# Splitting half of the second gated weight set on GpSimd, in a two-layer decoder trunk

## The chip, the cores and the metric

The kernel runs on one core of a Trainium2 chip. The metric is the device time of one execution in microseconds, the median of three runs. Engines are called PE (TensorE), ScalarE (ACT), VectorE (DVE), GpSimd (POOL) and SP (SyncE, which issues the DMAs).

## What is computed

A decoder trunk of depth 2 for one sequence of 512 tokens with 1024 features, in float32: a layer with a diagonal state-space mixer and an MLP, then a layer with dilated attention and an MLP. Each sub-layer is an RMS norm, a shift and scale that come from a condition vector `c`, the mixer, a gate and a residual add. The place of the change is the end of the first mixer:

```python
z = jax.nn.gelu(y).astype(u.dtype)              # y: the state-space output, 512 x 1024
val, gate = jnp.split(z @ w_glu, 2, axis=-1)    # w_glu: 1024 x 2048
return val * jax.nn.sigmoid(gate)               # then h = h + gate_c * this
# ada_chunks, for each sub-layer: jax.nn.silu(c) @ w + b   (w: 1024 x 3072)
```

## The kernel before, in words

**Products in three parts.** A float32 product is made of three matmuls in a rounded format: each operand is split in a high half (the value rounded, a cast) and a low half (the value less its high half). For weights, `weights` (L811) loads 128 x 8 x 256 raw values by DMA, casts them to the high half `wh` (L828, on ScalarE) and subtracts to the low half `wl` (L830, on VectorE). For the activations, L773 is the cast (ScalarE) and L778 the subtraction (VectorE, or GpSimd for units 1 and 2). `linear_steps` (L842) issues, for each of eight k, high x high (L856), high weight x low activation (L857) and low weight x high activation (L858).

**The state-space mixer** (`ssm`, from L1626 on) works on four units of the features. A unit's end is: outputs on PE (L747, L751), copies (L753, ScalarE), transposes (L767, PE), gelu (L770, two per half, ScalarE), L773, L778. Unit ft gives the activations k = ft and k = ft + 4. VectorE's scans are L719, with products L710 to L716 ahead and L729 to L733 behind; those of unit 3 are in part on GpSimd (L729, L730).

**The gated product** (`glu`, L935) uses eight *sets* of weights, each 128 columns for the value and 128 for the gate, in the order k = 0, 4, 1, 5, 2, 6, 3, 7. So the matmuls of units 0, 1, 2 and 3 come in this order. Each set takes two PSUM banks of four (`mm_ps`, L79), so set n + 2 takes the banks of set n, which the sigmoid (L945, ScalarE) and L956 (VectorE) have read. Behind each set VectorE works on *ada jobs* (L1523, L1530 seven times, L1535, L1536): parts of the product of `c` with the ada weights of the next sub-layers, each with its own load of 1 MB (L1512).

**The first three sets** are made ready before `glu` begins (L1762). For them `weights` works in quarters: quarter i is k = i and i + 4. Of the tuple, the number for a set says how many of its quarters are cast and split on GpSimd; the others follow, by a given order, behind the copies of unit 3's kernel on ScalarE and the scan of unit 3 on VectorE. The raw loads of these sets wait for a mark on PE. From set 4 on, ScalarE casts and VectorE subtracts in two halves of 128 x 1024.

**What sets the order.** Up to L1760 the engines' orders are pinned as written. Around and behind it a scheduler orders each engine's instructions by a model of their times, so a change in one place can move others. Raw weights, high and low halves and ada loads all take tiles from one pool of 13 buffers (`W`), so each load waits, on SP's queue and in SP's order, for whoever last used its buffer.

Names in the built program: set 1 is W_1651 (raw), W_1654 (high), W_1655 (low); set 2 is W_1664, W_1667, W_1668; set 3 W_1677, W_1680, W_1681; set 4 W_1831, W_1834, W_1835; set 5 W_1840, W_1843, W_1844; set 6 W_1932, W_1935, W_1936; set 7 W_2024, W_2027, W_2028. Unit 3's activations are uz_215, unit 1's uz_195.

Of the kernel before, what the change touches and what calls it, by code (L numbers as in the profile page):

```python
# [94 lines left out]
class Trunk:  # L95
# [1646 lines left out]
    def run(self):  # L1742
        nc, a = self.nc, self.a
        stop = getattr(self, "stop", None)
        self.jobs_started = False
        self.job_mark, self.heads = None, False
        self.jobs, self.ends, self.mark, self.pe_mark, self.pending = [], [], None, None, []
        self.late, self.loaded = [], None
        self.r, self.rcol, self.columns_only = [None] * 2, [None] * 2, False
        self.stream, self.ready = self.weight_stream(), []  # L1750
        self.setup()
        self.z = [None] * KT
        self.unit = [None] * 4
        pool, dve = nc.gpsimd, nc.vector
        self.ssm_params()
        with self.pinned():
            gate0 = self.ssm(pool, dve)

        def ada(n, c0, c1, late=False):

            return self.ada_jobs(a["ada_w"][n // 2, n % 2][:, c0 * D:c1 * D], (c1 - c0) * D, n, c0, late)
        self.prefetch(3, (2, 0, 0))  # L1762
        self.side(0)
        ada1 = ada(1, 0, 2)
        self.glu(gate0)
        if stop == "h1":
            return
        self.side_rest()
        gate1 = ada(1, 2, 3)
        adakv = self.ada_jobs(a["kv_ada_w"], 2 * D, None, 0)  # L1770
        ada2 = ada(2, 0, 2)
        self.mlp(0, ada1[:, 0:8], ada1[:, 8:16], gate1)
        if stop == "h2":
            return
        self.side_rest()
        self.masks()
        gate2, ada3, gate3 = ada(2, 2, 3, True), ada(3, 0, 2, True), ada(3, 2, 3, True)
        self.attention(ada2, adakv, gate2)
        if stop == "h3":
            return  # L1780
        self.columns_only = True
        self.mlp(1, ada3[:, 0:8], ada3[:, 8:16], gate3)
        if stop == "h4":
            return
        while len(self.pending) > 1:
            self.pump()
        self.final(1)[0]()
# [34 lines left out]
```

## Time and profile before

| | before |
|---|---|
| median of 3 runs | 1546.73 us (1542.74 to 1547.42) |
| the profiled execution | 1544.54 us, its span 1542.8 us |
| PE busy | 1466.8 us, 95% of the span |
| VectorE busy | 926.1 us, 60% |
| ScalarE busy | 569.5 us, 37% |
| GpSimd busy | 108.9 us, 7%, nearly all of it in the first 175 us |
| mean granted clock of PE | 0.987 |

A busy share is a mean over stages with different limits. In the first 140 us the state-space mixer keeps VectorE at work and PE waits often; from the gated product on PE is nearly always busy. In the timelines below a row is one group of equal instructions that follow each other: start, length, engine, line, operation, tiles, shape and count, and in brackets the idle time of the engine before it and what ended it. A clock of 1.00 is the higher of PE's two levels, 2.4 GHz, and 0.50 the lower.

### The profile page before, as it was taken

The numbers are of one execution on the slowest core, as the hardware profiler recorded it, in microseconds if no ns is written. First come the engines' busy times: TensorE is split into PE (matmuls) and PEld (weight loads), VectorE is DVE, ScalarE is ACT, GpSimd is POOL, SyncE is SP. The second block draws the span as 40 slices with busy tenths as digits, with TensorE's granted clock in tenths as the row PEclk, the third lists the DMA queues.
The fourth block names the chain that finished last, engine by engine and source line by source line (L and its number), as shares of the span: only waits on it lengthen the run. The fifth ranks groups of instructions, "written<-read, shape, count | busy, mean of one in ns | idle before, by whom it ended". The sixth has DMA issues, their size and how long they took to land. (4 is left out here: it accounts for less than half of the span.)

```text
span 1542.8 us, 27284 instructions
## 1 busy us (share of the span) xinstructions
PE 1466.8 (95%) x11654; PEld 1230.6 (80%) x11654; DVE 926.1 (60%) x1657; ACT 569.5 (37%) x990; POOL 108.9 (7%) x94
## 2 busy tenths in 40 slices
PE   4847899999999999999999999999999999999998
PEld 3636789888888888987987888888778888888887
DVE  7898896989874345636656756533558534334332
ACT  6738533424142234423322322332435423232222
POOL 7582000000000000000000000000000000000000
PEclk9978999999999999999999999999999999999999
DMA  9413671976743333233444444222334333232301
GB/s 216 152 55 84 198 221 40 323 228 191 228 135 107 104 116 96 82 88 114 139 129 144 138 125 143 83 56 72 117 91 135 94 98 109 82 110 84 107 1 55
DMA packets 214489, 188.61 MB, mean 122 GB/s; under 512 B 7480, under 2 KB 208352, under 8 KB 214368
## 3 DMA queue, kind: packets, MB, share of 16 engines
q1 hardware_dynamic: 214368, 186.87, 40.2%
q8 instruction: 91, 1.49, 0.4%
q14 instruction: 30, 0.25, 0.1%
HBM read 182.66 MB, written 4.19 MB: 121 GB/s over the span
## 5 line engine op out<-in xcount | busy, mean ns | idle before, releaser
L828 ACT CAST W<-W 128x1024 fp32r<-128x1024 f32 (+1 forms) x228 | 223.6, 1031 | 391.9 <-PE mm L857 204.3
L856 PE MATMUL mm<-uz,W 128*128 128x512 f32 (+1 forms) x952 | 360.0, 381 | 1.9 <-ACT uz L773 1.7
L858 PE MATMUL mm<-uz,W 128*128 128x512 f32 (+1 forms) x952 | 358.3, 377 | 3.1 <-DVE W L830 3.1
L857 PE MATMUL mm<-uz,W 128*128 128x512 f32 (+1 forms) x952 | 358.1, 376 | 3.2 <-DVE uz L778 2.9
L830 DVE TENSOR_TENSOR W<-W,W 128x1024 fp32r<-128x1024 f32 (+1 forms) x228 | 266.5, 1196 | 151.2 <-ACT W L828 122.8
L856 PE MATMUL mm<-hid,W 128*128 128x512 f32 (+1 forms) x792 | 298.7, 378 | 0.9 <-ACT hid L1029 0.6
L857 PE MATMUL mm<-hid,W 128*128 128x512 f32 (+1 forms) x792 | 296.1, 374 | 2.7 <-DVE hid L1030 2.7
L858 PE MATMUL mm<-hid,W 128*128 128x512 f32 (+1 forms) x792 | 295.4, 373 | 0.0
L858 PEld LDWEIGHTS mm<-uz,W 128*128 128x128 f32 x952 | 179.8, 189 | 36.2 <-DVE W L830 3.5
L856 PEld LDWEIGHTS mm<-uz,W 128*128 128x128 f32 x952 | 179.7, 189 | 35.9 <-ACT uz L773 2.1
L857 PEld LDWEIGHTS mm<-uz,W 128*128 128x128 f32 x952 | 179.8, 189 | 35.3 <-DVE uz L778 3.2
L857 PEld LDWEIGHTS mm<-hid,W 128*128 128x128 f32 x792 | 149.1, 188 | 29.4 <-DVE hid L1030 3.8
L856 PEld LDWEIGHTS mm<-hid,W 128*128 128x128 f32 x792 | 148.8, 188 | 28.8 <-issue 1.4
L858 PEld LDWEIGHTS mm<-hid,W 128*128 128x128 f32 x792 | 149.0, 188 | 26.6
L881 DVE SCALAR_TENSOR_TENSOR h<-mm,ada,h 128x512 f32<-128x512 f32 (+1 forms) x77 | 54.1, 707 | 148.4 <-PE mm L858 148.4
L1530 DVE SCALAR_TENSOR_TENSOR aacc<-W,cs,aacc 128x256 f32<-128x256 f32 x196 | 96.4, 492 | 4.0
L1056 ACT ACTIVATE sg<-mm 128x512 f32<-128x512 f32 x60 | 35.6, 595 | 112.9 <-PE mm L858 111.1
L1058 DVE TENSOR_TENSOR sg<-sg 128x512 f32<-128x512 f32 x64 | 43.7, 687 | 54.1 <-ACT uz L1057 53.9
L1282 PE MATMUL mm<-W,hid 128*128 128x256 f32 x256 | 73.5, 287 | 0.0
L1283 PE MATMUL mm<-W,hid 128*128 128x256 f32 x256 | 72.4, 283 | 0.0
L1284 PE MATMUL mm<-W,hid 128*128 128x256 f32 x256 | 72.4, 283 | 0.0
L1155 ACT ACTIVATE sg<-aux,st 128x192 f32<-128x192 f32 (+3 forms) x64 | 36.7, 577 | 96.2 <-DVE st L1153 96.1
(334 smaller groups left out, 1661.9 us busy)
## 6 DMA issues: line engine op xcount, KB each, us to landing
W<-in_mlp_w_dram SPq DMA_DIRECT2D x64, 1024.0 KB, 5.3
W<-in_ada_w_dram SPq DMA_DIRECT2D x20, 1024.0 KB, 6.1
h<-in_ada_w_dram SPq DMA_DIRECT2D x64, 256.0 KB, 3.1
W<-in_w_kv_dram SPq DMA_DIRECT2D x12, 1024.0 KB, 5.4
W<-in_w_kv_dram SPq DMA_DIRECT2D x24, 512.0 KB, 4.1
W<-in_attn_w_q_dram SPq DMA_DIRECT2D x24, 512.0 KB, 5.4
W<-in_ssm_w_glu_dram SPq DMA_DIRECT2D x16, 512.0 KB, 5.0
W<-in_kv_ada_w_dram SPq DMA_DIRECT2D x8, 1024.0 KB, 5.4
```

Source lines behind the costliest of these rows:

```text
L828: h = (nc.gpsimd.tensor_copy if first else nc.scalar.copy)(wh[:, ks], raw[:, ks])
L830: j = eng.tensor_tensor(wl[:, ks], raw[:, ks], wh[:, ks].bitcast(F32), ALU.subtract)
L856: nc.tensor.matmul(o, wh[:, k], uh, start=(start and k == order[0]), stop=False)
L857: nc.tensor.matmul(o, wh[:, k], ul, start=False, stop=False)
L858: self.pe_mark = nc.tensor.matmul(o, wl[:, k], uh, start=False, stop=(stop and k == order[-1])).ins
L881: self.mark = nc.vector.scalar_tensor_tensor(self.h[k][:, cs], src[:, cs], gate[:, k:k + 1], self.h[k][:, cs], ALU.mult, ALU.add).ins
L1058: nc.vector.tensor_tensor(rl, rl, rl, ALU.mult)
L1155: self.act_mark = nc.scalar.activation(p[:, 0:W], ps[:, 0:W], AF.Exp, bias=st[:, 1, e:e + 1], scale=0.125, accum_out=st[:, 2, e:e + 1]).ins
L1282: nc.tensor.matmul(ps[:, j], us[0], wh, start=(k == 0), stop=False)
L1283: nc.tensor.matmul(ps[:, j], us[0], wl, start=False, stop=False)
L1284: nc.tensor.matmul(ps[:, j], us[1], wh, start=False, stop=(k == KT - 1))
L1530: i = nc.vector.scalar_tensor_tensor(acc, raw[k], self.cs[:, k:k + 1], acc, ALU.mult, ALU.add)
```

## The change

```diff
-        self.prefetch(3, (2, 0, 0))
+        self.prefetch(3, (2, 2, 0))
```

Two of the four quarters of set 2 (k = 0, 4 and k = 1, 5) are cast and split on GpSimd, behind those of set 1; ScalarE and VectorE keep the other two. In `weights` these two quarters then also have no order against ScalarE's and VectorE's marks. The scheduler moves other instructions with it.

GpSimd, difference at the end of the mixer (W_1654 and W_1655 set 1, W_1667 and W_1668 set 2, uz_195 unit 1's activations):

```order
 L828 CAST W_1654<-W_1651 128x2x256 x2
 L830 TENSOR_TENSOR W_1655<-W_1651,W_1654 128x2x256 x2
+L828 CAST W_1667<-W_1664 128x2x256 x2
+L830 TENSOR_TENSOR W_1668<-W_1664,W_1667 128x2x256
 L778 TENSOR_TENSOR uz_195_1408<-W_572,uz_195_1408 128x512 x2
+L830 TENSOR_TENSOR W_1668<-W_1664,W_1667 128x2x256
 L729 TENSOR_TENSOR rstd_1565<-W_1237,hid_491 128x8x63
 L730 TENSOR_TENSOR rstd_1566<-W_1237,hid_490 128x8x63
```

Four instructions are added, one of the subtractions behind unit 1's L778.

ScalarE, difference from set 4's casts to the first sigmoid (hid_1093 is unit 3's gelu output, sg_1742 the sigmoid of set 1):

```order
 L828 CAST W_1834<-W_1831 128x1024 x2
 L770 ACTIVATE hid_1093<-aux_1632 128x4x64 x2
+L828 CAST W_1843<-W_1840 128x1024 x2
 L770 ACTIVATE hid_1093<-aux_1639 128x4x64 x2
 L773 CAST uz_215_1646<-hid_1093 128x512 x2
-L828 CAST W_1843<-W_1840 128x1024 x2
+L828 CAST W_1935<-W_1932 128x1024 x2
 L945 ACT_TABLE_LOAD
 L945 ACTIVATE sg_1742<-mm_1693 128x512
```

Set 5's casts moved between unit 3's two pairs of L770, and set 6's casts moved ahead of the table load and the first sigmoid; they stood behind two sigmoids and two L901.

VectorE, difference where it splits sets 4 and 5 beside the second ada job (aacc_1812):

```order
 L830 TENSOR_TENSOR W_1835<-W_1831,W_1834 128x1024
 L1530 SCALAR_TENSOR_TENSOR aacc_1812<-W_1810,cs_78,aacc_1812 128x256
 L830 TENSOR_TENSOR W_1835<-W_1831,W_1834 128x1024
-L1530 SCALAR_TENSOR_TENSOR aacc_1812<-W_1810,cs_78,aacc_1812 128x256
-L778 TENSOR_TENSOR uz_215_1646<-hid_1093,uz_215_1646 128x512 x2
-L1530 SCALAR_TENSOR_TENSOR aacc_1812<-W_1810,cs_78,aacc_1812 128x256 x2
+L1530 SCALAR_TENSOR_TENSOR aacc_1812<-W_1810,cs_78,aacc_1812 128x256 x5
 L830 TENSOR_TENSOR W_1844<-W_1840,W_1843 128x1024
 L1535 STREAM_TRANSPOSE W_1810<-aacc_1812 128x256
 L830 TENSOR_TENSOR W_1844<-W_1840,W_1843 128x1024
 L1536 TENSOR_REDUCE apart_1690<-W_1810 128x8
```

Unit 3's L778 moved from the middle of that ada job to behind its L1536. On SP the order is the same, but of two loads the buffers are others: set 6's raw weights and the ada load ahead of them (W_1914) now take buffers that VectorE's second ada job and its second subtraction of set 5 give back.

## Rows read from the trace of the kernel before

**Rows 1.** Busy time by stretch; then PE's granted clock, DMA share, GB/s.

```profile
160.00:162.00 2.00, 1.58 (x4) 1.29 (x5) 2.00 (x4) 0.00 (x0) 0.00 (x0) 0.50 0.43 100
...
185.00:200.00 15.00, 15.00 (x67) 12.40 (x67) 13.69 (x26) 5.10 (x7) 0.00 (x0) 1.00 1.11 319
```

**Rows 2.** Timeline of PE, 145 to 185 us.

```profile
145.29 0.50 PE L857 MATMUL mm<-uz,W 128*128 128x512 f32 x1 [2.87 <-DVE uz L778]
...
160.42 0.80 PE L858 MATMUL mm<-uz,W 128*128 128x512 f32 x1 [3.09 <-DVE W L830]
...
163.48 0.39 PE L856 MATMUL mm<-uz,W 128*128 128x512 f32 x1
...
166.47 1.03 PE L767 MATMUL aux<-cst,W 128*128 128x128 f32 x8
...
176.21 1.04 PE L767 MATMUL aux<-cst,W 128*128 128x128 f32 x8
...
180.41 0.40 PE L857 MATMUL mm<-uz,W 128*128 128x512 f32 x1
...
184.96 0.45 PE L856 MATMUL mm<-uz,W 128*128 128x512 f32 x1
```

**Rows 3.** Timeline of GpSimd, 133 to 149 us.

```profile
133.12 2.18 POOL L828 CAST W<-W 128x512 fp32r<-128x512 f32 x2 [21.98 <-DMA W<-in_ssm_w_glu_dram]
135.27 3.86 POOL L830 TENSOR_TENSOR W<-W,W 128x512 fp32r<-128x512 f32 x2
146.37 2.52 POOL L778 TENSOR_TENSOR uz<-W,uz 128x512 fp32r<-128x512 f32 x2 [7.25 <-ACT uz L773]
```

**Rows 4.** Timeline of VectorE, 133 to 185 us.

```profile
133.26 3.11 DVE L719 TENSOR_TENSOR_SCAN W<-sqs,W 128x512 f32<-128x512 f32 x2
...
137.94 1.73 DVE L729 TENSOR_TENSOR sg<-W,hid 128x504 f32<-128x504 f32 x1
...
139.59 0.67 DVE L730 TENSOR_TENSOR sg<-W,hid 128x504 f32<-128x504 f32 x1
...
149.97 2.33 DVE L719 TENSOR_TENSOR_SCAN W<-sqs,W 128x512 f32<-128x512 f32 x2
...
158.48 6.10 DVE L830 TENSOR_TENSOR W<-W,W 128x512 fp32r<-128x512 f32 x10
164.50 0.35 DVE L1523 TENSOR_SCALAR aacc<-W,cs 128x256 f32<-128x256 f32 x1
...
169.34 0.34 DVE L1523 TENSOR_SCALAR aacc<-W,cs 128x256 f32<-128x256 f32 x1
...
179.37 1.29 DVE L778 TENSOR_TENSOR uz<-hid,uz 128x512 fp32r<-128x512 f32 x2 [3.10 <-ACT uz L773]
...
184.09 0.41 DVE L1536 TENSOR_REDUCE apart<-W 128x8 f32<-128x256 f32 x1
```

**Rows 5.** Timeline of ScalarE, 176 to 195 us.

```profile
176.84 2.06 ACT L770 ACTIVATE hid<-aux 128x256 f32<-128x256 f32 x4 [3.17 <-PE aux L767]
...
181.76 1.28 ACT L945 ACT_TABLE_LOAD   x1
184.25 0.60 ACT L945 ACTIVATE sg<-mm 128x512 f32<-128x512 f32 x1 [1.21 <-PE mm L858]
...
192.90 2.00 ACT L828 CAST W<-W 128x1024 fp32r<-128x1024 f32 x2 [3.95 <-DMA W<-in_ssm_w_glu_dram]
```

**Rows 6.** Timeline of SP's issues, 132 to 187 us.

```profile
132.30 0.99 SPq L818 DMA_DIRECT2D W<-in_ssm_w_glu_dram  x2
...
170.97 0.99 SPq L818 DMA_DIRECT2D W<-in_ssm_w_glu_dram  x2
...
184.02 0.37 SPq L1512 DMA_DIRECT2D W<-in_ada_w_dram  x1
184.48 1.96 SPq L818 DMA_DIRECT2D W<-in_ssm_w_glu_dram  x2
```

**Rows 7.** Median time to landing of the two issues at 170.97; count, size, us.

```profile
W<-in_ssm_w_glu_dram SPq DMA_DIRECT2D x2, 512.0 KB, 4.7
```

## The prediction

> **What bounds the kernel now.** I read the busy times by stretch first: from 185 to 200 us the matrix engine (PE) is busy 15.00 of 15.00 us, and the table of waits of PE for 185 to 600 us is empty [rows 1]. So a microsecond taken out of PE's way before 185 us is worth a microsecond at the end, and a gap put into the gap-free part costs its length. Next I read PE's timeline from 140 us, where the change acts: PE waits 2.87 us for VectorE's L778 until 145.29, and 3.09 us for VectorE's L830, the low half of a split, until 160.42; set 3 begins at 184.96 without a gap [rows 2]. Last come the timelines of the engines beside it and SP's issues [rows 3 to 6].
>
> The wait that ends at 160.42 has a plain cause. Set 2's matmuls need its low half, and VectorE makes that in a run of ten L830 that begins at 158.48 [rows 4]: two for set 1, four for set 2, four for set 3. Behind the wait the granted clock is 0.50, the lower of its two levels (1.2 GHz), after PE had stood still [rows 1]. Seven matmuls take 160.42 to 163.48, 3.06 us; the twenty from 180.41 to 184.96 take 0.228 each [rows 2], so seven would take 1.6. Stall and low clock hold 3.1 + 1.4 = 4.5 us.
>
> **The change, part by part.** *GpSimd* gets two casts L828 and two subtractions L830 of set 2. Set 1's cost 2.18 and 3.86 us there and end at 135.27 + 3.86 = 139.13 [rows 3]. Set 2's raw weights are issued from 132.30 on in two pieces. Of such a pair (median 4.7 us to landing, the first 4.1, so the second 5.3, and issued some 0.6 later) the last has landed 5.9 us behind the first issue [rows 6, 7]: 138.2. So both casts and one subtraction run from 139.13 to 139.13 + 2.18 + 1.93 = 143.24, inside GpSimd's gap of 7.25 us that ends at 146.37; the two L778 keep their place, and the last subtraction runs from 148.9 to 150.9, while the next GpSimd work waits for VectorE's scans of unit 3 (149.97, 2.33 for the two) [rows 3, 4]. GpSimd's own gap hides all of it; without it, PE would wait for GpSimd instead (rival c).
>
> *VectorE beside it.* It loses two L830 of 6.10/10 = 0.6 us: a gain of 1.2. But while GpSimd ran set 1, two scans took 3.11 instead of 2.33 us, and L729 took 1.73 where L730, of the same size and beside an idle GpSimd, took 0.67 [rows 4]: 1.8 us, and 2.2 with a third operation there that was slowed less. No row shows set 2's work beside this part of VectorE, so I bound its price: 0, if its operations miss each other, and 4.1 us, if VectorE stands for all of 139.13 to 143.24. I take 2.2, the nearest row, 1.6 of it ahead of L778.
>
> The Trainium skill (SBUF — State Buffer, "Who interferes with whom") says that a VectorE instruction with two inputs in SBUF and a GpSimd instruction that reads SBUF exclude each other for a whole instruction. The L729 agrees, which ends 0.5 us behind GpSimd's L830 instead of beside it; the scans beside the casts agree only in part. By the rule the price would be the upper bound, and the result about 2 us later than mine.
>
> *PE up to set 2's end.* L857 gets VectorE's L778 1.6 us later. The stall of 4.5 us is gone, since GpSimd's low halves are there at 150.9. So PE is at the transposes of unit 2 at 166.47 - 4.5 + 1.6 = 163.6, and at those of unit 3 at 176.21 - 2.9 = 173.3 [rows 2]: 2.9 us ahead. This is the gain of the change.
>
> *What it meets on ScalarE and VectorE.* In the new order the casts of set 5 (two L828, 2.00 us, as set 6's at 192.90 [rows 5]) stand between the two pairs of L770 on ScalarE; they stood behind L773. Their weights are issued behind unit 3's output matmuls, at 170.97 before and 168.1 now, and land 5.9 us later [rows 6, 7], 174.0, while the first pair of L770 runs; so they cost only their length. L770 starts 0.63 us behind the transposes (176.21, 176.84) and L773 lets VectorE's L778 go 2.53 later (179.37) [rows 2, 4, 5]; now that is 173.3 + 0.6 + 2.5 + 2.0 = 178.4. But VectorE is later still. From 164.50, behind the ten L830, to 184.50 (184.09 + 0.41) it has 20.0 us, of which 3.1 are the wait for L773 and 1.2 L778 [rows 4]; the other 15.7 now all stand ahead of L778. They start at 164.5 + 2.2 - 1.2 = 165.5 and end at 181.2. L778 comes then, where it came at 179.37: the gain is eaten, and PE ends set 2 some 1.8 us later than before, at about 186.8.
>
> *The new stall.* The first matmul of set 3 takes the PSUM bank that the sigmoid L945 of set 1 reads. Before, that sigmoid ran from 184.25 to 184.85, just ahead of 184.96 [rows 2, 5]. Now set 6's two casts and the table load stand ahead of it on ScalarE, and the casts need set 6's raw weights. Before, they stood behind both sigmoids and waited 3.95 us for their DMA, until 192.90, with nobody behind them [rows 5]. The DMA can't go much sooner: on SP's queue it stands behind an ada load whose buffer VectorE's second L830 of set 5 frees, now at 181.2 less one L1536, 180.8, and it waits itself for that L1536, 181.2. Before, the ada load was issued at 184.02, set 6's pieces at 184.48 and 185.06, and the casts could start at 192.90 [rows 5, 6], 8.9 us behind the first. So now: landed 180.9 + 8.9 = 189.8; casts 2.00, 191.8; table load 1.28 [rows 5], 193.1; sigmoid 0.60, 193.7; PE 193.8. The casts' own buffer is freed by an ada job of 4.8 us (164.50 to 169.34 [rows 4]) behind L778: 182.5 + 4.8 = 187.3, so that isn't last. PE stands from 186.8 to 193.8. Set 3 starts 193.8 - 184.96 = 8.8 us late, and the low clock behind such a stall costs 1.4 again. Sum: +10.2 us. What follows is PE without gaps, in the same order from the last weight pair on, so it stays to the end. Each later sigmoid also stands behind the casts of one set further on, but PE asks for those a whole set (48 matmuls, 11 us) later: covered.
>
> Bounds of the landing: 5.9 us from set 6's own issue (181.3) if the ada load doesn't delay it; then the ada job, 187.3, decides, 2.5 earlier. With a VectorE price of 0 the chain is 2.2 earlier; both leave +5.5. With 4.1 it is 2 later: +12.2.
>
> The profiled execution takes 1544.54 us (span 1542.8), the median of three is 1546.73. From the first, +10.2 gives 1554.7; from the median, with which the result is compared, 1556.9. I say 1557.
>
> **Rivals.** (a) *Same: the sigmoid isn't held.* Set 6's weights land by 183; only VectorE's queue counts, and PE reaches set 3 1.8 us late: 1548.5, at most 2 us either way. For it: in the same chain set 5's casts find their weights in time. Against it: set 6's casts waited for theirs until 192.90 before. (b) *Faster: the removed stall stays removed.* GpSimd's work costs VectorE nothing, L778 isn't late, the sigmoid isn't held: 1546.73 - 4.5 = 1542.2. For it: the gap is real, and GpSimd is empty beside it. It needs set 6's weights by 178, some 12 us sooner than I work out and before their buffer is free. (c) *A stall on GpSimd besides*: its first subtraction runs past 146.37 and holds up L778 there, and PE waits for GpSimd near 155. It decides if the casts start 3 us late, and would add about 2: 1559. Against it: the landing at 138.2.
>
> **How the numbers follow.** Forecast (slower by 5.5 to 12.2) 0.74, (a) 0.15, (b) 0.06, (c) 0.05. A change of under 0.3%, 4.6 us, can hardly be told from none in this kernel's runs (1542.74 to 1547.42). Slower by over 0.3%: the forecast and (c) but for low runs, 0.77. Within: (a) and those, 0.16. Faster: (b) and a lucky (a), 0.07. The range leaves out (b) and most of (a): from 1548.5, which takes in the low ends and the spread of runs, to 1561, which takes in 4.1 for VectorE, and (c) and the spread.
>
> **What would show it.** Right: no PE wait for L830 near 158; GpSimd busy from 139 to 143; PE's wait for VectorE's first L778 ending near 146.9 instead of 145.29; PE 2 to 3 us early at the transposes of units 2 and 3; then a new wait of PE for L945 of about 7 us that ends near 194, with ScalarE waiting for the gated-weight DMA ahead of it, and a clock of 0.5 behind it; nothing new after that. Wrong: PE without a gap between 181 and 200, or set 6's casts before 184 us. Then it is the sign that is wrong, not the size.

## The result, and the profile after

The changed kernel takes 1555.49 us (median of four runs, 1553.15 to 1556.05); the kernel before, run beside it, 1544.95 (1542.74 to 1547.42, four runs). The ratio is 1.0065, with a 95% interval of 1.0047 to 1.0084: slower by 10 us, 7 to 13. Ratios here and below are taken over all fast executions of both kernels, so they are not the quotients of the two medians. The profiled execution has a span of 1553.2 us against 1542.8. Below, "PE's transposes of unit 1" are the eight L767 at 135.16 before and 135.19 after: up to there the two traces agree to 0.2 us.

PE's timeline after, beside [rows 2]; the number in brackets is how long PE stood still, and what released it:

```profile
146.85 0.80 PE L857 MATMUL mm<-uz,W 128*128 128x512 f32 x1 [4.66 <-DVE uz L778]
...
156.40 0.25 PE L1576 MATMUL aux<-apart,cst 128*32 128x8 f32 x8
...
164.88 1.04 PE L767 MATMUL aux<-cst,W 128*128 128x128 f32 x8
...
174.64 1.03 PE L767 MATMUL aux<-cst,W 128*128 128x128 f32 x8
...
179.72 1.32 PE L856 MATMUL mm<-uz,W 128*128 128x512 f32 x4 [3.58 <-ACT uz L773]
181.55 0.79 PE L857 MATMUL mm<-uz,W 128*128 128x512 f32 x1 [0.50 <-DVE uz L778]
...
188.72 0.39 PE L858 MATMUL mm<-uz,W 128*128 128x512 f32 x1
193.40 0.50 PE L856 MATMUL mm<-uz,W 128*128 128x512 f32 x1 [4.29 <-ACT sg L945]
```

Three things are to be seen. The wait for L830 at 160.42 is gone, and PE is at unit 2's transposes at 164.88 instead of 166.47: 1.6 us ahead. By the end of set 2 (188.72 + 0.23, before 184.96) it is 4.0 us behind. And set 3 begins at 193.40 instead of 184.96, 8.4 us late, behind a wait of 4.29 us for the sigmoid. The sigmoid after that comes at 206.22 instead of 196.12, 10.1 us late, and the last output at the end 10.4.

ScalarE's timeline after, beside [rows 5]:

```profile
175.28 1.18 ACT L770 ACTIVATE hid<-aux 128x256 f32<-128x256 f32 x2 [1.73 <-PE aux L767]
176.22 2.02 ACT L828 CAST W<-W 128x1024 fp32r<-128x1024 f32 x2
178.12 1.12 ACT L770 ACTIVATE hid<-aux 128x256 f32<-128x256 f32 x2
179.01 1.18 ACT L773 CAST uz<-hid 128x512 fp32r<-128x512 f32 x2
189.45 1.99 ACT L828 CAST W<-W 128x1024 fp32r<-128x1024 f32 x2 [9.26 <-DMA W<-in_ssm_w_glu_dram]
191.46 1.28 ACT L945 ACT_TABLE_LOAD   x1
192.75 1.09 ACT L945 ACTIVATE sg<-mm 128x512 f32<-128x512 f32 x2
```

Set 5's casts (176.22) stand between the pairs of L770 and cost their 2.0 us there. Set 6's casts wait 9.26 us for their transfer, and the table load and both sigmoids wait behind them in order. PE had finished the inputs of both sigmoids at 189.11 (188.72 + 0.39), 3.6 us before the first one starts.

GpSimd after, beside [rows 3]:

```profile
139.17 1.86 POOL L828 CAST W<-W 128x512 fp32r<-128x512 f32 x2 [0.17 <-DMA W<-in_ssm_w_glu_dram]
140.99 1.70 POOL L830 TENSOR_TENSOR W<-W,W 128x512 fp32r<-128x512 f32 x1
146.19 3.42 POOL L778 TENSOR_TENSOR uz<-W,uz 128x512 fp32r<-128x512 f32 x2 [3.51 <-ACT uz L773]
149.58 1.28 POOL L830 TENSOR_TENSOR W<-W,W 128x512 fp32r<-128x512 f32 x1
```

VectorE after, beside [rows 4]:

```profile
139.47 1.08 DVE L730 TENSOR_TENSOR sg<-W,hid 128x504 f32<-128x504 f32 x1
140.58 2.64 DVE L733 TENSOR_TENSOR W<-sg,sg 64x504 f32<-64x504 f32 x2
...
144.57 1.37 DVE L733 TENSOR_TENSOR W<-sg,sg 64x504 f32<-64x504 f32 x2
...
146.11 2.37 DVE L778 TENSOR_TENSOR uz<-W,uz 128x512 fp32r<-128x512 f32 x2
...
160.50 4.89 DVE L830 TENSOR_TENSOR W<-W,W 128x512 fp32r<-128x512 f32 x8
...
180.48 0.41 DVE L1536 TENSOR_REDUCE apart<-W 128x8 f32<-128x256 f32 x1
180.81 1.28 DVE L778 TENSOR_TENSOR uz<-hid,uz 128x512 fp32r<-128x512 f32 x2
```

GpSimd's four instructions lie in the gap, and the instructions that VectorE runs beside them are longer: L730 1.08 us instead of 0.67, the pair of L733 2.64 where the same pair at 144.57, beside an idle GpSimd, takes 1.37. That is 1.7 us ahead of L778. The clock by stretches (the third number from the right is PE's granted clock):

```profile
148.00:150.00 2.00, 1.97 (x6) 1.18 (x5) 2.00 (x4) 1.95 (x5) 2.00 (x2) 0.50 0.10 23
150.00:152.00 2.00, 2.00 (x6) 1.30 (x4) 2.00 (x5) 1.94 (x6) 0.86 (x1) 0.50 0.95 285
...
182.00:184.00 2.00, 2.00 (x6) 1.52 (x6) 1.86 (x6) 0.00 (x0) 0.00 (x0) 0.50 0.95 321
```

Behind the wait of 4.66 us, and again behind the 3.58 us at 179.72, PE runs at the lower level (1.2 GHz). Before, 150 to 152 and 182 to 184 us had a clock of 1.00.

### The profile page after: what moved, and what is told of

Read it like the earlier page. It is cut to its first block, busy times and chain, and to the rows that moved or that the text cites. A ratio compares the mean times of both kernels' runs of the same rounds, so it can differ in the third digit from the quotient of the medians.

```text
span 1553.2 us, 27290 instructions
## 1 busy us (share of the span) xinstructions
PE 1470.8 (95%) x11654; PEld 1233.8 (79%) x11654; DVE 928.0 (60%) x1655; ACT 568.5 (37%) x988; POOL 114.7 (7%) x98
## 5 line engine op out<-in xcount | busy, mean ns | idle before, releaser
L857 PE MATMUL mm<-uz,W 128*128 128x512 f32 (+1 forms) x952 | 360.2, 379 | 5.6 <-DVE uz L778 5.2
L830 DVE TENSOR_TENSOR W<-W,W 128x1024 fp32r<-128x1024 f32 (+1 forms) x226 | 265.1, 1201 | 153.3 <-ACT W L828 129.6
L857 PE MATMUL mm<-hid,W 128*128 128x512 f32 (+1 forms) x792 | 296.2, 374 | 2.7 <-DVE hid L1030 2.7
L857 PEld LDWEIGHTS mm<-uz,W 128*128 128x128 f32 x952 | 180.9, 190 | 39.2 <-DVE uz L778 6.8
L857 PEld LDWEIGHTS mm<-hid,W 128*128 128x128 f32 x792 | 149.2, 188 | 29.5 <-DVE hid L1030 3.8
```

Of the source, the lines that this page charges most:

```text
L830: j = eng.tensor_tensor(wl[:, ks], raw[:, ks], wh[:, ks].bitcast(F32), ALU.subtract)
L857: nc.tensor.matmul(o, wh[:, k], ul, start=False, stop=False)
```

## The experiments

My theory was that the loss sits on ScalarE: the new order puts casts that wait for a transfer ahead of L773 and of the table load. The main rival was that GpSimd's extra work itself, by what it takes from VectorE, is the loss. The table gathers what the experiments gave, each against the kernel before, run beside it. "Set 3" is the start of set 3's sigmoid in the profiled execution, counted from that execution's transposes of unit 1 and compared with the 60.96 us before (196.12 - 135.16): the others reach these transposes up to 2.8 us before or after it does, and a count from there leaves that out. Each of these counts is of one execution.

```
kernel                                        set 3     ratio    95% interval
the change                                    +10.1 us  1.0065   1.0047 to 1.0084
A  set 5's casts back behind L773              -1.4     0.9997   0.9983 to 1.0011
B  set 6's casts back behind the sigmoid       +2.5     1.0030   1.0018 to 1.0042
C  ada load behind set 6's load                +6.0     1.0039   1.0026 to 1.0051
D  A, and set 2 on GpSimd behind L778          -1.6     0.9991   0.9976 to 1.0005
E  the new order without the change            +7.6     1.0063   1.0040 to 1.0086
F  D, and set 4's casts behind L773            -1.5     0.9984   0.9968 to 0.9999
G  before, and set 4's casts behind L773       -0.4     1.0002   0.9986 to 1.0017
H  F, and VectorE's ada job behind L778        -4.2     0.9963   0.9949 to 0.9978
```

An "order" in the edits is one between two instructions of the same engine: it adds no wait on another engine.

**A. Set 5's casts back behind L773.**

```diff
-            nc.scalar.copy(uz[:, 2 * s], z[s])
+            self.uz_mark = nc.scalar.copy(uz[:, 2 * s], z[s]).ins
...
+            self.after(h.ins, behind) if behind is not None else None   # behind: self.uz_mark for set 5
```

> The change as it is, but ScalarE does set 5's casts behind unit 3's last L773, as before the change; ScalarE then has its old order from there on, with set 6's casts behind the sigmoids too. My theory (what the change loses, it loses on ScalarE, where casts that wait for a transfer now stand ahead of L773 and of the table load): no wait of 3.6 us at unit 3's products and none of 4.3 us at set 3; the 1.6 us won at unit 2's transposes are kept, set 3 starts at about 183.4 and the time is 1543.3, 1542 to 1544.5. Rival (GpSimd's extra work beside VectorE is the loss: the longer wait for VectorE's L778 at 146.85 and the low clock behind it): set 3 still starts late and the time stays at 1549 or more.

Measured: 1545.41 us against 1544.93, ratio 0.9997 (0.9983 to 1.0011). ScalarE in A:

```profile
178.82 1.16 ACT L773 CAST uz<-hid 128x512 fp32r<-128x512 f32 x2
179.88 2.01 ACT L828 CAST W<-W 128x1024 fp32r<-128x1024 f32 x2
181.90 1.28 ACT L945 ACT_TABLE_LOAD   x1
184.59 0.60 ACT L945 ACTIVATE sg<-mm 128x512 f32<-128x512 f32 x1 [1.41 <-PE mm L858]
...
190.88 2.00 ACT L828 CAST W<-W 128x1024 fp32r<-128x1024 f32 x2 [1.72 <-DMA W<-in_ssm_w_glu_dram]
```

Set 6's casts have gone back behind the sigmoids too, with only set 5's ordered, and VectorE's L778 of unit 3 no longer stands behind set 5's L830. The sigmoid waits for PE again, as before. PE's wait for L773 is 1.70 us, as before, and none for L945 is left. GpSimd's work and the wait behind it at VectorE's L778 (4.89 us) are still there, so the rival falls: with the order back, the whole loss is gone. What I had the wrong size of is the gain. The profile shows 1.4 us at set 3's sigmoid, but the time is no shorter that can be measured: the interval goes from 2.6 us faster to 1.7 slower.

**B. Set 6's casts alone back behind the sigmoid.** The same edit, with set 6 ordered behind the second sigmoid, and set 5 left between the L770.

> The change as it is, but ScalarE does set 6's casts behind the second sigmoid; set 5's stay where the change puts them, between unit 3's L770. My theory (two separate losses on ScalarE: 4.0 us by the end of set 2 from L773 being late, then 4.3 us from set 6's casts): set 2 ends at about 189 as in the changed kernel, no wait for L945 stands at set 3, and the time is 1549, 1547.5 to 1551. Rival (one loss only, the transfer of set 6, which makes whatever uses it late wherever the cast stands): the wait moves to set 6's own products and the time stays at 1553 to 1556. Rival (GpSimd's price is the loss): 1553 to 1556 too.

Measured: 1549.93 us, ratio 1.0030 (1.0018 to 1.0042). PE in B has no wait for L945; what it has at unit 3's products is

```profile
179.55 2.00 PE L856 MATMUL mm<-uz,W 128*128 128x512 f32 x4 [3.96 <-ACT uz L773]
```

So there are two losses, as the theory has it: set 5's casts ahead of L773 cost 2.5 us at the sigmoid of set 3 in this one profile and 2.8 to 6.5 us of time by the ratio, and the rest, 7.6 of the 10.1 us in the profile, goes with set 6's casts ahead of the sigmoid. That split is by difference. Behind unit 3's transposes PE's only wait here is the one for L773, though VectorE's L778 stands behind the ada job as in the changed kernel; so ScalarE's order holds PE up here, and not VectorE's.

**C. The ada load behind set 6's loads.** All else as in the change; ScalarE's order too.

```diff
-            self.side(1 if ob < 2 else 2)
+            self.side(1 if ob < 3 else 2)
```

> The change as it is, but the loop over the gated sets does two ada jobs a step only from its fourth set on, so that the second ada load of that stretch is issued behind set 6's two loads and not ahead of them. ScalarE still casts set 6 ahead of the table load. My theory (set 6's landing ends the wait of 4.3 us, and it is late because it queues behind the ada load): set 6 lands about 4 us earlier, near 185.5, its casts end near 187.5 and the sigmoid near 189.5, so that set 3 starts at 189 to 190 instead of 193.4 and the time is 1551, 1549 to 1553. Rival (the landing is set by the buffer that comes free or by set 6's own transfer, not by the load ahead): set 6 lands at 189 as now and the time stays at 1554 to 1557.

Measured: 1551.51 us, ratio 1.0039 (1.0026 to 1.0051). ScalarE in C, and SP's issue of set 6's two loads, first in the changed kernel and then in C:

```profile
181.08 2.04 SPq L818 DMA_DIRECT2D W<-in_ssm_w_glu_dram  x2
...
179.85 1.00 SPq L818 DMA_DIRECT2D W<-in_ssm_w_glu_dram  x2
...
185.76 2.00 ACT L828 CAST W<-W 128x1024 fp32r<-128x1024 f32 x2 [6.83 <-DMA W<-in_ssm_w_glu_dram]
187.78 1.28 ACT L945 ACT_TABLE_LOAD   x1
189.08 1.09 ACT L945 ACTIVATE sg<-mm 128x512 f32<-128x512 f32 x2
```

From the transposes of unit 1, the casts start at 51.8 us (185.76 - 133.97) instead of 54.3 (189.45 - 135.19) in the changed kernel: 2.5 us sooner, not 4. PE's wait for L945 goes from 4.29 to 1.71 us. The landing is what the sigmoid waits for. The loads are issued at the same point in both, 45.9 us behind those transposes, so the 2.5 us lie wholly between issue and landing: the casts start 8.4 us behind the issue with the ada load ahead, and 5.9 without. What sets the time of the issue is the other part of the delay, and C leaves it as it was.

**E. The new order without the change.** The split on GpSimd is that of before, (2, 0, 0), but ScalarE is held to the changed kernel's order from unit 3's L770 on.

```diff
+            self.after(self.gelus[-2], h.ins) if self.nset == 5 else None   # second pair of L770 behind set 5's casts
+            self.after(self.sigs[0], h.ins) if self.nset == 6 else None     # first sigmoid behind set 6's casts
```

> The kernel before, with set 2 left wholly to ScalarE and VectorE (no change on GpSimd), but ScalarE is held to the changed kernel's order: set 5's casts between unit 3's L770, set 6's ahead of the table load and the first sigmoid. VectorE then takes set 5's L830 ahead of unit 3's L778, as in the changed kernel. My theory (the loss is this order alone): set 6's casts wait for their transfer until about 190 to 192, set 3 starts at 193 to 196 instead of 185, and the time is 1556, 1553 to 1559, at least as late as the changed kernel, since nothing is won at unit 2's transposes. Rival (the order costs something only together with GpSimd's extra work, which makes the casts or the transfers late): 1549 or less.

Measured: 1553.43 us against 1546.06, ratio 1.0063 (1.0040 to 1.0086): a loss that can't be told from that of the changed kernel, with nothing changed on GpSimd. In the one profile it is smaller, 7.6 us against 10.1, and set 3 starts at 189.35 where I expected 193 to 196. PE in E:

```profile
143.62 0.50 PE L857 MATMUL mm<-uz,W 128*128 128x512 f32 x1 [2.93 <-DVE uz L778]
...
158.12 0.50 PE L858 MATMUL mm<-uz,W 128*128 128x512 f32 x1 [2.49 <-DVE W L830]
...
179.22 2.08 PE L856 MATMUL mm<-uz,W 128*128 128x512 f32 x4 [3.56 <-ACT uz L773]
...
189.35 0.80 PE L856 MATMUL mm<-uz,W 128*128 128x512 f32 x1 [2.86 <-ACT sg L945]
```

The first two waits are those of before [rows 2], the last two those of the changed kernel. One difference: here set 6's casts, at 185.39, are released by PE's L857 and not by the DMA, and the wait for L945 is 2.86 us. No ada load is issued right ahead of set 6's loads here: they are issued at 179.22, and with C's 5.9 us to landing they would land at 185.1, an estimate. So landing and buffer lie close together in E, and E lacks the later landing of the changed kernel, which goes with its smaller loss in the profile. VectorE's L778 moves with ScalarE's order in E as in A, but PE has no wait for it here either.

**D. GpSimd's half of set 2 behind unit 1's L778.** Beside A's order, GpSimd's casts of set 2 are ordered behind its L778 of unit 1, and its L729 of unit 3 behind set 2's last subtraction.

```diff
+            self.after(h.ins, self.lo_mark[1]) if first and self.nset == 2 else None
...
+            self.after(self.rotd[3], j.ins) if first and self.nset == 2 else None
```

> Like the kernel with set 5's casts behind L773, and GpSimd does its half of set 2 only behind unit 1's L778, ahead of unit 3's L729: nothing of set 2 runs on GpSimd beside VectorE's scans, L730 and L733 at 133 to 144. My theory (GpSimd's work there costs VectorE 1.6 us ahead of unit 0's L778, and the PE wait at 146.85 grew by that): that wait is back at 2.9 us, the gain at unit 2's transposes grows from 1.6 to about 3, set 3 starts near 181.9, and the time is 1541.8, 1540.5 to 1543. Rival (VectorE's slower instructions come from something else than GpSimd's work beside them): the wait stays at 4.7 us and the time is that of the kernel with set 5's casts behind L773. Third way (set 2's low parts come late, at 153 to 155, as PE reaches them at 154): a new wait of 1 to 3 us there, and 1543 to 1546.

Measured: 1542.75 us, ratio 0.9991 (0.9976 to 1.0005), not to be told from before. PE's wait at the first L778:

```profile
141.80 0.50 PE L857 MATMUL mm<-uz,W 128*128 128x512 f32 x1 [2.40 <-DVE uz L778]
...
171.18 1.73 PE L856 MATMUL mm<-uz,W 128*128 128x512 f32 x4 [2.83 <-ACT uz L773]
```

and VectorE in D, where GpSimd now works:

```profile
145.89 1.09 DVE L716 TENSOR_TENSOR W<-sg,W 128x512 f32<-128x512 f32 x1
146.91 3.79 DVE L719 TENSOR_TENSOR_SCAN W<-sqs,W 128x512 f32<-128x512 f32 x2
...
154.04 2.33 DVE L733 TENSOR_TENSOR W<-sg,sg 64x504 f32<-64x504 f32 x2
```

The wait at L778 is back to 2.40 us, so GpSimd's work did cost VectorE the 1.6 to 1.8 us there. But the price went with the work: the two scans of unit 3, which take 2.33 us beside an idle GpSimd [rows 4], now take 3.79. PE meets unit 2's transposes much sooner (its order changed too: they now stand ahead of set 2's last products), then waits 2.83 us for L773, because set 4's casts stand ahead of unit 3's L770, and runs at half clock from 172 to 178. What was won goes there. Not all of D's lead at set 3 is due to the edit: behind its first wait, of 2.40 us, the clock stayed at 1.00, and the work up to L1576 took 6.4 us, where before it took 7.9. VectorE, GpSimd and ScalarE have the same order in both up to that wait, so this is a difference between two executions.

**F and G. Set 4's casts behind L773 too.** F is D with set 4 ordered like set 5; G is the kernel before with sets 4 and 5 ordered so.

> Like the kernel in which GpSimd does its half of set 2 behind unit 1's L778, with one step more: ScalarE does set 4's casts behind unit 3's last L773 too, and not ahead of unit 3's L770. In that kernel set 4's casts (166.78, behind a wait of 4.37 us) end at 168.7 and hold L770 back by 1 us, PE waits 2.83 us for L773 at 171.18, and its clock is at half from 172 to 178. My theory (that wait and the low clock behind it give back what the earlier start won): the wait goes below 1.8 us, the clock stays up, set 3 starts some 3 us earlier against the kernel with only set 5's casts moved, and the time is 1540, 1538 to 1542. Rival (set 4's casts and low parts are then too late for set 4's own products, or push set 5's and set 6's): a wait at set 4 and 1543 to 1547.

> The kernel before, nothing changed on GpSimd, with set 4's and set 5's casts on ScalarE behind unit 3's last L773. My theory (before the change unit 3's L770 waits for PE's transposes and not for set 4's casts, so moving these wins nothing by itself): no difference, 1545, 1543.5 to 1546.5. Rival (set 4's casts ahead of unit 3 cost time in the kernel before as well): 1541 to 1543. Third way (set 4's casts come too late): 1547 or more.

Measured: F 1542.43 us against 1546.06, ratio 0.9984 (0.9968 to 0.9999); G 1546.67, ratio 1.0002 (0.9986 to 1.0017). G shows no difference, as expected: by itself this move wins nothing. F's median lies above its range of 1538 to 1542. The wait for L773 is 1.70 us there, but PE then stands still for VectorE, and the clock does not stay up:

```profile
171.73 1.19 PE L856 MATMUL mm<-uz,W 128*128 128x512 f32 x4 [1.70 <-ACT uz L773]
...
175.58 0.79 PE L857 MATMUL mm<-uz,W 128*128 128x512 f32 x1 [2.66 <-DVE uz L778]
...
172.00:174.00 2.00, 0.92 (x4) 0.40 (x3) 1.86 (x5) 2.00 (x3) 0.00 (x0) 0.79 0.00 0
174.00:176.00 2.00, 0.42 (x1) 0.42 (x2) 1.96 (x5) 1.36 (x2) 0.00 (x0) 0.50 0.00 0
```

The mechanism of my expectation failed here: one wait gave way to the next.

**H. VectorE's ada job behind L778.** F, and VectorE's second ada job ordered behind unit 3's last L778.

```diff
             i = nc.vector.tensor_scalar(acc, raw[0], self.cs[:, 0:1], None, ALU.mult)
+            self.njob += 1; self.after(i.ins, self.lo_mark[3]) if self.njob == 2 else None
```

> Like the kernel with GpSimd's half of set 2 behind unit 1's L778 and with set 4's and set 5's casts behind unit 3's last L773, with one step more: VectorE starts its second ada job (L1523 and seven L1530) only behind unit 3's L778, which in that kernel stood behind the job's first seven instructions and ended at 175.5, while its input was there at 171.7. My theory (PE's wait of 2.66 us for L778 at 175.58 and the half clock from 173 to 179 behind it are what is left of the loss): L778 ends at about 172.5, that wait goes below 0.5 us, the clock stays up, set 3 starts 4 to 5 us earlier, and the time is 1538, 1536 to 1540.5. Rival (the later ada job brings the next loads and so set 5's and set 6's casts late): a new wait at sets 3 to 6, and 1541 to 1545.

Measured: 1541.40 us against 1545.51, ratio 0.9963 (0.9949 to 0.9978): faster than the kernel before by 5.7 us (3.4 to 7.9; the medians differ by 4.1), and so faster than the changed kernel. PE in H, which waits for nothing between 174.27 and 215 us:

```profile
144.52 0.50 PE L857 MATMUL mm<-uz,W 128*128 128x512 f32 x1 [3.10 <-DVE uz L778]
...
171.08 1.04 PE L767 MATMUL aux<-cst,W 128*128 128x128 f32 x8
174.27 1.20 PE L856 MATMUL mm<-uz,W 128*128 128x512 f32 x4 [1.69 <-ACT uz L773]
```

The clock is 1.00 in every stretch from 150 to 200 us. The rival fails: no new wait stands at sets 3 to 6. But the forecast for H was 1538, with a range to 1540.5, and the median is 3.4 above it. Set 3's sigmoid is 2.7 us sooner than in F by the table's count, less than the 4 to 5 forecast. The rest was lost ahead of the edit. From unit 1's transposes to unit 3's PE takes 36.80 us in H (134.28 to 171.08) and 34.48 in F (134.05 to 168.53), 2.3 more: 0.7 because the first wait ends later and 1.6 by a low clock behind it, 7.95 us to L1576 against 6.36. Up to that wait the two have the same order on VectorE, GpSimd and ScalarE, so F's execution had the better start, and 2.7 + 2.3 = 5.0 us is what the edit shows. Moreover the profiled execution of H, the slowest of its nine, loses 2.9 us of its lead between the first and the last L1272 (636 and 1010 us before), in the attention, where nothing was changed: PE's waits for VectorE's L1160 from 640 to 1180 us are 5.7 us in sum, 4.0 before. The executions of A, B and G lose 1.1, 2.5 and 2.5 there. Why it varies I have not tried.

No run has H's orders without the work on GpSimd. But from unit 1's transposes to unit 3's the kernel before takes 41.05 us, so H is 4.25 ahead there, before the reordered casts on ScalarE and the moved ada job begin; at set 3's sigmoid it is 4.2 ahead. G, with the casts' order and without the split, takes 40.70 and still waits 2.49 us for VectorE's L830. So the lead comes from the stall that GpSimd's half of set 2 took out, and H's orders keep it.

## Why the prediction was right, step by step

The predicted 1557 us stands against 1555.5 measured; +10.2 in the sum against +10.4 of span. The mechanism was the one forecast, and rivals (a), (b) and (c) fall: the sigmoid is held, and GpSimd's L778 began at 146.19, no later than before, with no wait of PE for GpSimd behind it. (Set 2's weights let GpSimd start at 139.17, not at 138.2 as forecast, so it waited 0.17 us for them.) Inside the sum two terms were mis-sized. Both make PE later at the end of set 2, 189.0 instead of 186.8, and neither reaches the time, since set 3 waits for a landing that comes later still.

- *Stall and low clock taken out: 4.5 predicted.* From L1576 to unit 2's transposes PE takes 8.48 us (156.40 to 164.88), before 13.26 (153.21 to 166.47): 4.8. Right.
- *VectorE's price ahead of L778: 1.6 predicted.* The L857 that waits for it starts at 146.85 instead of 145.29. Right, from L730 and one pair of L733. The Trainium skill has the rule (SBUF — State Buffer, "Who interferes with whom") that a VectorE instruction with two inputs in SBUF and a GpSimd instruction that reads SBUF exclude each other for a whole instruction. The trace agrees. GpSimd's second cast of set 2 ends at 141.03 and its first subtraction at 142.69; the two L733 that began beside them take 0.97 and 1.66 us and end at 141.55 and 143.22, 0.5 us behind each. What failed is the prediction's working from the rule: it had VectorE stand for all of 139.13 to 143.24. By the rows VectorE stands only for what is left of the GpSimd instruction under way when its own begins, and that came to 1.7 us beside 3.5 us of GpSimd. So by the rule, too, the result does not come 2 us later than the forecast.
- *Gain at unit 2's transposes: 2.9 predicted, 1.6 measured.* This is the first term that failed: the longer wait at L778 has a longer low clock behind it. From the released L857 to L1576 PE takes 9.55 us, before 7.92 (145.29 to 153.21). I had counted the wait's growth and nothing behind it.
- *L773 and L778 of unit 3 late, set 2's end at 186.8 predicted; 189.0 measured.* L778 came at 180.81 (181.2 forecast). But PE also stood 3.58 us for L773 (1.68 before) and then ran at a low clock: 0.66 from 180 to 182 us, 0.50 to 186, 0.63 to 188. From 179.72 to the end it took 9.2 us, before 5.6 (179.39 to 184.96). That low clock was not in the sum. This is the second term.
- *Set 6's landing: 189.8 predicted, its casts start at 189.45; set 3 at 193.8 predicted, 193.40 measured.* Right. The chain is casts 1.99, table load, sigmoid, as laid out. Because PE arrives later than thought, the wait shows as 4.29 us and not as 7.0, but the start of set 3 is fixed by the landing, so the two errors ahead of it did not reach the time. B and C confirm both ends of this link: without the casts ahead, PE doesn't wait for L945; with an earlier landing it waits 2.6 less. C also bears out the bound of 5.9 us from issue to landing without the ada load, 2.5 sooner.
- *Low clock behind the new wait: 1.4 predicted.* The delay grows from 8.4 at the start of set 3 to 10.1 at its sigmoid: 1.7.

The cause is the order on ScalarE and what came behind it: E has the loss without the change, A has the change without the loss. VectorE's order moved along in both; in B and E, where it stands as in the changed kernel, PE waits for ScalarE alone.

## What to carry to other kernels

A change on one engine is priced by what the instruction order of the others becomes: read for each in-order engine which instruction now stands behind one that waits for a transfer, and when that transfer lands. Once PE has slack ahead of such a point, what is last there decides the time, and gains and losses before it don't show; so put the casts that wait behind the instructions PE needs, and only then give work away. When one wait is taken out, look for the next on the same product (here L773, then L778), since the gain came only when all of them were gone.

## What the runs showed of the hardware

How much of the lower clock follows a wait differed by more than I had expected. PE's work from the L857 that waits for VectorE's first L778 to L1576 is the same in all these kernels. It took 6.4 us behind waits of 2.40 and 2.60 us (D, F), with a granted clock of 1.00 throughout in both; 7.9 to 8.0 behind 2.87 to 3.16 (before, E, G, H); and 9.1 to 9.6 behind 4.64 to 4.89 (the change, A, B, C). So a wait of 4.7 us cost up to 3 us behind it that one of 2.4 did not. The wait is not all that counts: 2.60 and 2.87 us lie close together, with 1.6 us between what followed (F and before); and in F a wait of 2.66 us at 175.58, with one of 1.70 us just ahead of it, did have half clock behind it.

Where VectorE and GpSimd met, one stood until the other's instruction had ended, and only where both inputs of VectorE's lay in SBUF. Beside GpSimd's two L778 of unit 1 [rows 3], which end at 148.89, VectorE had in the kernel before

```profile
147.55 0.68 DVE L714 TENSOR_TENSOR sg<-mm,hid 128x512 f32<-128x512 f32 x1
148.15 1.29 DVE L715 TENSOR_TENSOR W<-W,sg 128x512 f32<-128x512 f32 x1
```

L714, one of whose inputs is in PSUM (mm), took as long as ever. L715 ended 0.55 us behind GpSimd. In D GpSimd's first subtraction ends at 149.63 and VectorE's second scan at 150.70, one scan's length behind it. It goes both ways: GpSimd's and VectorE's L778, which ran one after the other before, meet after the change (146.19 and 146.11) and take turns, and both pairs grow: 2.52 to 3.42 and 1.29 to 2.37 us.
